# A transformer block in float32 parts: three quarters of a feed-forward product by seven products for eight

## The chip, the core and the metric

The kernel runs on one core of a Trainium2 chip. The metric is the time of one execution on the device in microseconds (us), the median of several runs.

## What is computed

Two layers of a hybrid block on 512 tokens of 1024 features, and after them two more mixers (a latent attention and a gated linear recurrence) that the change doesn't touch. A layer of the block, cut to what matters here:

```python
mixed = ga * (ya @ w_proj_att) + gb * (yb @ w_proj_mlstm)
x = x + mixed @ w_out
h2 = rms_norm(x, norm_mlp_w)
x = x + jnp.square(jax.nn.relu(h2 @ w_ff1)) @ w_ff2
```

Here ya is the output of a dilated attention and yb that of an mLSTM. w_ff1 is 1024 x 4096, w_ff2 is 4096 x 1024. The second feed-forward product, the last line's right one, is what the change rewrites.

## The kernel before, in words

All large products are made exact enough by parts. A float32 operand v becomes hi + lo, two float32r tiles: ScalarE copies v to hi, VectorE subtracts (`split`, lines 246 and 247). A product is then three matmuls, hi hi, hi lo and lo hi (`mm3`, lines 275 to 277). Each has 128 x 128 stationary elements and mostly 512 moving columns, and adds up in a bank of PSUM.

Weights come as units of 128 x 1024 float32, 512 KB, in the order in which they are used (`stream`, line 252). SP loads a unit into one of two tiles `raw` (line 259), and a split puts its parts into one of four tiles `spl`.

There are two shapes of product. A "tall" one keeps a weight unit still and moves the activations: 8 k x 3 = 24 matmuls give 128 features of all 512 tokens, in one bank A. A "wide" one keeps 128 tokens of an activation still and moves 512 columns of weights: `add_wide` (line 733) calls `halves` and `wide_acc`, and for each of two column halves and four token tiles 4 k x 3 = 12 matmuls fill a bank A, which VectorE adds into the residual x (line 737). There are two banks A; the attention uses three S, two T and one O besides.

The feed-forward stage of a layer runs over blocks b of 512 hidden features. For b below 8 there are four tall steps: one unit of w_ff1 each, relu on ScalarE (line 678), square on VectorE (line 679), and a split into `fs[b]`, a tile `big` of 16 KB a partition. After the first block each turn also does the wide product of block b - 1, 96 matmuls and four units of w_ff2. Between them stand uses of the modulation (lines 812 to 819): three VectorE sums over a unit of other weights that ScalarE's queue loads, 24 a layer.

The tiles `big` have five places. big0 to big2 lie in a pool that outlives the block and is opened on the left side of the on-chip memory; big3 and big4 lie in the pool `rest`, opened on the right side, so at its far end. fs uses the places 3, 4, 2 in turn; ya and yb lie in 3 and 4. The residual x, `raw`, `spl` and the constants are opened first, on the left.

Nobody writes the order of the work out by hand. The program lists it, and a planner lays each engine's queue down once, by the order of the program and its own estimate of what is ready and which places are free; on the chip each queue then runs in that order and waits on semaphores. Work without a place to wait for can so move far ahead: the modulation runs well before the feed-forward stage in which it is listed.

Of the kernel before, what the change touches and what calls it, by code (L numbers as in the profile page):

```python
# [24 lines left out]
# column groups of w_in  # L25
C_AQ, C_AK, C_AV, C_MQ, C_MK, C_MV, C_MO = (512 * i for i in range(7))
C_MI = 3584
C_GA, C_GB = 3592, 4616


# ------------------------------------------------------------------ host layout

def _tall(w, c0, n=128):
# [15 lines left out]
def pack_layer(a, l):  # L49
# [12 lines left out]
    for b in range(9):  # L62
        if b < 8:
            u += [_tall(f1, 512 * b + 128 * j) for j in range(4)]
        if b:
            for ch in range(2):
                u += [_wide(f2, 4 * (b - 1) + k, 512 * ch) for k in (0, 2)]
    return np.stack(u)

# [20 lines left out]
    # two heads' columns without position; four heads' that turn, first halves before second ones  # L90
# [36 lines left out]
def constants():  # L127
    i = np.arange(128)
    c = {"ident": np.eye(128, dtype=np.float32)}
    # multiplicity of a key at distance d in the three dilated patterns, as a logarithm  # L130
# [29 lines left out]
def layout(a):  # L160
    m = {}
    for l in range(2):
        m[f"wl{l}"] = pack_layer(a, l)
        m[f"cl{l}"] = pack_cols(a, l)
# [21 lines left out]
# ------------------------------------------------------------------ the program  # L186
# [5 lines left out]
class Prog:  # L192
    def __init__(self, tc, A, ctx):
        self.tc, self.nc, self.A, self.ctx = tc, tc.nc, A, ctx
        self.const = self.pool("const", 1)
        self.res = self.pool("res", 1)
        self.raw = self.pool("raw", 2)
# [15 lines left out]
    def rows(self, pool, ap, n, name, **kw):  # L213
        """A row of DRAM on every partition."""
# [4 lines left out]
    def psum(self, st, **banks):  # L219
        """Pools of PSUM: name -> (tiles, banks of a tile)."""  # L220
# [21 lines left out]
    # exact parts: x = hi + lo, each in float32r  # L242
# [47 lines left out]
def rms(P, dst, x, row, junk):  # L290
    """dst = x / rms(x) row"""
# [6 lines left out]
def act_of(tiles):  # L298
    """k -> (hi, lo) of a split, transposed activation kept four k to a tile."""
# [3 lines left out]
def trig_tables(P, ck):  # L303
    """sin and cos of the rope: token on partitions, [4 token tiles, 8 heads, 8 frequencies]."""
    nc = P.nc
    pos = P.load(ck, "pos", [128, 4], "pos", I32)
    inv = P.load(ck, "k_inv", [128, 8], "inv")
    posf = ck.tile([128, 4], F32, name="posf")
    nc.vector.tensor_copy(posf, pos)
    ang = ck.tile([128, 2, 4, 8], F32, name="ang")  # L310
# [6 lines left out]
    rn = ck.tile([128, 2, 4, 8], F32, name="rn")  # L317
# [14 lines left out]
def first_block(P, xs, pool):  # L332
# [1176 lines left out]
```

## Time and profile before

| what | us |
|---|---|
| median of 3 runs | 2382.06 |
| lowest, highest run | 2379.44, 2382.68 |
| span of the profiled execution, first to last instruction | 2376.0 |
| TensorE busy | 2336.0 |
| VectorE busy | 1438.8 |
| ScalarE busy | 961.2 |
| GpSimd busy | 48.5 |

The profile is of one execution; of its own time the span is what it records, and 6.1 us lie between that span and the median of the runs. Busy time counts an engine as busy from the start to the end of each instruction. Matmuls overlap, so their durations add up to more than they cost: the distance between two starts is the price of one. The feed-forward stages, from the first relu of line 678 to the last addition into x of line 737, are at about 440 to 792 us and 1217 to 1577 us.

### The profile page before, as it was taken

The page shows a single profiled execution, that of the slowest core. Times are in us where ns is not written, and L with a number is a line of the kernel's source. Part 1 is how long each engine was busy: PE and PEld are TensorE (multiplying, and loading weights), DVE is VectorE, ACT ScalarE, POOL GpSimd, SP SyncE. Part 2 cuts the span into 40 slices and gives each one's busy share as a digit, 9 for nine tenths or more (in the row PEclk, how much of TensorE's full clock was granted, in tenths as well). Part 3 has the DMA queues.
Part 4 walks back from the last instruction along what each step waited for, and adds up shares of the span by engine and source line. Part 5 has one row for each costly group of instructions (what it writes and reads, how often), then busy time and mean ns, then how long its engine had stood idle before and what let it go on. Part 6 is the DMA issues. An engine that isn't in the chain of part 4 may idle for free.

```text
span 2376.0 us, 30969 instructions
## 1 busy us (share of the span) xinstructions
PE 2336.0 (98%) x12280; PEld 1904.2 (80%) x12280; DVE 1438.8 (61%) x2534; ACT 961.2 (40%) x1809; POOL 48.5 (2%) x96
## 2 busy tenths in 40 slices
PE   8999999999999999999999999999999999999998
PEld 6777888888888777788888888789888888788886
DVE  4477795544444547779654444454477776647486
ACT  3356422422322226642342232333366783363332
POOL 0000000000000000000000000010000000000000
PEclk9999999999999999999999999999999999999999
DMA  4221463222323222146432222312110130121111
GB/s 152 80 82 48 166 215 124 92 94 89 106 89 99 83 80 72 54 152 215 136 106 98 89 98 98 97 39 89 45 28 19 24 88 22 59 88 36 48 51 71
DMA packets 61345, 209.24 MB, mean 88 GB/s; under 512 B 8576, under 2 KB 9872, under 8 KB 60944
## 3 DMA queue, kind: packets, MB, share of 16 engines
q1 hardware_dynamic: 54000, 179.99, 23.4%
q10 hardware_dynamic: 7200, 27.27, 3.5%
q8 instruction: 97, 1.59, 0.3%
q14 instruction: 48, 0.39, 0.1%
HBM read 201.99 MB, written 2.10 MB: 86 GB/s over the span
## 4 chain that ended last, share of the span: by engine, by line
PE 84%; DVE 8%; ACT 3%; DMA 2%; issue 2%; POOL 1%; SPq 0%; ACTq 0%; POOLq 0%; DVEq 0%
PE A L277 22%; PE A L276 22%; PE A L275 21%; PE O L1133 2%; PE T L1125 2%; DVE spl L247 2%; PE S L275 1%; PE O L512 1%; PE S L276 1%; PE S L277 1%; PE S L486 1%; DMA ada<-in_ada 1%; PE T L506 1%; DVE junk L817 1%; ACT spl L246 1%
## 5 line engine op out<-in xcount | busy, mean ns | idle before, releaser
L246 ACT ACTIVATE spl<-raw 128x1024 fp32r<-128x1024 f32 (+2 forms) x313 | 325.0, 1040 | 477.0 <-PE A L277 429.6
L275 PE MATMUL A<-big,spl 128*128 128x512 f32 (+1 forms) x1280 | 483.0, 377 | 1.9 <-DVE x L737 1.2
L277 PE MATMUL A<-big,spl 128*128 128x512 f32 (+1 forms) x1280 | 481.4, 376 | 0.2 <-DVE spl L247 0.2
L276 PE MATMUL A<-big,spl 128*128 128x512 f32 (+1 forms) x1280 | 480.8, 376 | 0.0
L247 DVE TENSOR_TENSOR spl<-raw,spl 128x1024 fp32r<-128x1024 f32 (+2 forms) x313 | 375.8, 1204 | 163.1 <-ACT spl L246 161.7
L276 PE MATMUL A<-spl,big 128*128 128x512 f32 (+2 forms) x992 | 384.7, 389 | 1.1 <-DVE spl L247 1.0
L275 PE MATMUL A<-spl,big 128*128 128x512 f32 (+2 forms) x992 | 383.6, 388 | 1.6 <-ACT big L246 0.8
L277 PE MATMUL A<-spl,big 128*128 128x512 f32 (+2 forms) x992 | 381.8, 385 | 0.2 <-DVE ms L284 0.2
L277 PEld LDWEIGHTS A<-big,spl 128*128 128x128 f32 x1280 | 241.1, 188 | 45.9 <-issue 2.6
L275 PEld LDWEIGHTS A<-big,spl 128*128 128x128 f32 x1280 | 241.2, 188 | 45.1 <-DVE x L737 1.6
L276 PEld LDWEIGHTS A<-big,spl 128*128 128x128 f32 x1280 | 241.2, 188 | 43.3 <-issue 1.4
L275 PEld LDWEIGHTS A<-spl,big 128*128 128x128 f32 x992 | 186.3, 188 | 44.2 <-ACT big L246 2.8
L276 PEld LDWEIGHTS A<-spl,big 128*128 128x128 f32 x992 | 186.7, 188 | 40.3 <-DVE spl L247 3.0
L277 PEld LDWEIGHTS A<-spl,big 128*128 128x128 f32 x992 | 186.6, 188 | 39.2 <-issue 1.5
L737 DVE SCALAR_TENSOR_TENSOR x<-A,x 128x512 f32<-128x512 f32 x160 | 110.0, 688 | 121.7 <-PE A L277 119.9
L679 DVE TENSOR_TENSOR r<-r 128x512 f32<-128x512 f32 (+1 forms) x72 | 45.5, 633 | 170.9 <-ACT r L678 170.9
L678 ACT ACTIVATE r<-A 128x512 f32<-128x512 f32 (+1 forms) x72 | 39.7, 551 | 219.8 <-PE A L277 219.6
L1100 DVE TENSOR_REDUCE mx<-S 128x1 f32<-128x768 f32 (+1 forms) x80 | 71.8, 900 | 26.7 <-PE S L277 25.8
L1126 ACT ACTIVATE pt<-T 128x512 f32<-128x512 f32 (+1 forms) x144 | 66.5, 501 | 32.2 <-PE T L1125 31.1
L286 POOL TENSOR_TENSOR rstd<-ms,mhalf 128x1 f32<-128x1 f32 (+2 forms) x68 | 42.4, 623 | 1765.1 <-DVE ms L284 1720.8
L1105 ACT ACTIVATE p<-S,mx 128x768 f32<-128x768 f32 (+1 forms) x96 | 72.6, 760 | 13.8 <-DVE mx L1100 12.9
L817 DVE SCALAR_TENSOR_TENSOR junk<-ada,cond 128x512 f32<-128x512 f32 x96 | 65.7, 687 | 6.1 <-DMA ada<-in_ada 4.9
(413 smaller groups left out, 3438.8 us busy)
## 6 DMA issues: line engine op xcount, KB each, us to landing
raw<-in_wl SPq DMA_DIRECT2D x244, 512.0 KB, 3.2
ada<-in_ada ACTq DMA_DIRECT2D x48, 512.0 KB, 3.8
raw<-in_gla SPq DMA_DIRECT2D x33, 512.0 KB, 3.2
raw<-in_mla SPq DMA_DIRECT2D x20, 512.0 KB, 3.3
raw<-in_mla SPq DMA_DIRECT2D x8, 384.0 KB, 2.9
qT<-rot SPq DMA_DIRECT2D x32, 96.0 KB, 2.8
x<-in_x SPq DMA_DIRECT2D x4, 512.0 KB, 10.2
big<-in_wl SPq DMA_DIRECT2D x4, 512.0 KB, 9.3
```

What stands on the lines that cost most here:

```text
L246: nc.scalar.activation(hi, src, AF.Copy)
L247: nc.vector.tensor_tensor(lo, src, f32(hi), op=OP.subtract)
L275: mm(ps, lh, rh, start=start, stop=False)
L276: mm(ps, lh, rl, start=False, stop=False)
L277: mm(ps, ll, rh, start=False, stop=stop)
L737: P.nc.vector.scalar_tensor_tensor(xv, ps, scale, xv, op0=OP.mult, op1=OP.add)
L817: nc.vector.scalar_tensor_tensor(junk, w[:, o], 0.5, self.cond[:, 0, o], op0=OP.mult, op1=OP.mult, accum_out=self.acc[:, g, j:j + 1])
L1100: nc.vector.tensor_reduce(mx[:, 0:two], pss[:, 0:two * m].rearrange("p (t n) -> p t n", t=two), AX.X, OP.max, negate=True)
L1105: nc.scalar.activation(p[:, t * m:(t + 1) * m], pss[:, t * m:(t + 1) * m], AF.Exp, bias=mx[:, t:t + 1], accum_out=sl[:, t:t + 1])
L1125: nc.tensor.transpose(pst[:, k:k + 128], p[:, o + k:o + k + 128], P.ident)
L1126: nc.scalar.activation(pt[:, o:o + w], pst[:, 0:w], AF.Copy)
L1133: nc.tensor.matmul(weigh.o[64 * i:64 * i + 64, (t0 + t) * 128:(t0 + t + 1) * 128], V[4 * c + k][:, h * 64:(h + 1) * 64], pts[i][:, t * m + ...
```

## The change

In the first 3072 of the 4096 hidden features, six of the eight blocks, two blocks and all 512 tokens make a chunk. A chunk is a product of a 2 x 2 matrix of activation quarters (256 tokens by 512 features: a11, a12, a21, a22) with a 2 x 2 matrix of weight quarters (512 by 512, 1 MB: b11 and so on). The new class `Seven` computes it by seven products of sums of quarters. The activation sums are VectorE's (`total`). The weight sums are made where the quarter lies, by DMAs that GpSimd issues and that add to what is there (`accum_op`), four a chunk. The sums of products that are shared are kept in the banks S and O: X and Y are two banks each, products are added to what they hold, and VectorE adds each state of a bank to its place in x with a sign. SP loads four quarters a chunk into four places, in turn.

The activations stay as float32 when the features are made (relu and square both on ScalarE); a product splits the sum that it takes (`part`), and its two weight units, as it needs them. Feature steps and products alternate: a tall step, then one of the seven products of the chunk before. The last two blocks stay as wide products, with four activation parts. Each tall step of the first three of a group of four also lists one use of the modulation.

The pools move: x and `raw` go to the right side, the pool `rest` with big3 and big4 to the left, closed before the feed-forward stage, where `parts`, `quarter` and `hidden` take its place. The buffer for GpSimd's DMA descriptors is set to 1024 bytes a partition.

```diff
@@ pack_layer, pack_quarters
-    for b in range(9):
-        if b < 8:
-            u += [_tall(f1, 512 * b + 128 * j) for j in range(4)]
-        if b:
-            for ch in range(2):
-                u += [_wide(f2, 4 * (b - 1) + k, 512 * ch) for k in (0, 2)]
+    u += [_tall(f1, 128 * j) for j in range(32)]
+    for b in (6, 7):
+        for ch in range(2):
+            u += [_wide(f2, 4 * b + k, 512 * ch) for k in (0, 2)]
     return np.stack(u)
+def pack_quarters(a, l):
+    w = a["w_ff2"][l][0:3072].reshape(3, 2, 4, 128, 2, 512).transpose(0, 1, 4, 3, 2, 5)
+    return np.stack([w[:, i, j] for i, j in QUARTERS], axis=1).reshape(12, 128, 2048)
...
@@ Prog
-        self.res = self.pool("res", 1)
-        self.raw = self.pool("raw", 2)
+        self.res = self.pool("res", 1, side="right")
+        self.raw = self.pool("raw", 2, side="right")
...
@@ mm3
-    def mm3(self, ps, lh, ll, rh, rl, start, stop):
+    def mm3(self, ps, lh, ll, rh, rl, start, stop, **more):
         mm = self.nc.tensor.matmul
-        mm(ps, lh, rh, start=start, stop=False)
-        mm(ps, lh, rl, start=False, stop=False)
-        mm(ps, ll, rh, start=False, stop=stop)
-    # ---- residual stream -> normalised, transposed, split
+        mm(ps, lh, rh, start=start, stop=False, **more)
+        mm(ps, lh, rl, start=False, stop=False, **more)
+        mm(ps, ll, rh, start=False, stop=stop, **more)
...
@@ act_of, cut
+def cut(a):
+    return lambda t, k: tuple(v[:, t * 128:(t + 1) * 128] for v in a(k))
...
@@ first_block, pools
-    rest = P.pool("big", 1, st, side="right")
-    def big(i, dtype=F32R):
-        """Five places, three of them in the pool that outlives this block."""
-        return (pool if i < 3 else rest).tile([128, 2, 4, 512], dtype, name="big", tag=f"big{i}")
-    vp = P.pool("vp", 1, st)
-    tmp = P.pool("tmp", 2, st)
-    one = P.pool("one", 1, st)
-    pp = P.pool("pp", 3, st)
-    ck = P.pool("ck1", 1, st)
+    ck = P.pool("ck1", 1, st, side="right")
+    vp = P.pool("vp", 1, st, side="right")
     for l in range(2):
+        mixing = ExitStack()
+        rest = P.pool("big", 1, mixing)
+        tmp, one, pp = (P.pool(n, k, mixing) for n, k in (("tmp", 2), ("one", 1), ("pp", 3)))
+        def big(i, dtype=F32R):
+            return (pool if i < 3 else rest).tile([128, 2, 4, 512], dtype, name="big", tag=f"big{i}")
...
@@ first_block, feed-forward
+        mixing.close()
+        mod.start(l, vp)
         act2 = act_of(norm.dst)
-        mod.start(l, vp)
-        fs = {}
-        for b in range(9):
-            if b < 8:
-                fs[b] = big((3, 4, 2)[b % 3])
-                ws = [W() for _ in range(4)] if b == 0 else None
-                for n0, n1 in ((0, 256), (256, 512)) if b == 0 else ((0, 512),):
+        after = ExitStack()
+        parts = P.pool("parts", 3, after)
+        quarter, hid = P.pool("quarter", 1, after), P.pool("hidden", 1, after)
+        tmp, one = (P.pool(n, k, after) for n, k in (("tmp2", 3), ("one2", 1)))
+        seven = Seven(P, xs, A[f"wq{l}"], parts, quarter, tmp)
+        def features(c):
+            f = fs[c] = big(2, F32) if c % 2 == 0 else hid.tile([128, 2, 4, 512], F32, name="hidden")
+            for i in range(2):
+                ws = [W() for _ in range(4)] if c + i == 0 else None
+                for n0, n1 in ((0, 256), (256, 512)) if c + i == 0 else ((0, 512),):
                     for j in range(4):
                         ps = P.bankA()
                         tall(ps, ws[j] if ws else W(), act2, range(8), n0, n1)
-                        r = tmp.tile([128, 512], F32, name="r", tag="yf")[:, n0:n1]
+                        r = f[:, i, j, n0:n1]
                         nc.scalar.activation(r, ps[:, n0:n1], AF.Relu)
-                        nc.vector.tensor_tensor(r, r, r, op=OP.mult)
-                        P.split(fs[b][:, 0, j, n0:n1], fs[b][:, 1, j, n0:n1], r)
-            for g in range(24 * b // 9, 24 * (b + 1) // 9):
-                mod.use(l, g, tmp, "u")
-            done = None
-            if b == 7 and l == 1:
-                # what the mixer after this block takes of ctx
+                        nc.scalar.activation(r, r, AF.Square)
+                        yield
+        fs, chunks = {}, iter(range(24))
+        for c in range(4):
+            more = seven.chunk(c - 1, fs[c - 1]) if c else iter(())
+            for i, _ in enumerate(features(c)):
+                if i % 4 < 3:
+                    for g in itertools.islice(chunks, 1):
+                        mod.use(l, g, vp, "junk")
+                next(more, None)
+            for _ in more:
+                pass
+        for g in chunks:
+            mod.use(l, g, vp, "junk")
+        last = [[seven.part(seven.of(fs[3], i, j), *((quarter, "quarter1") if i + j == 2 else ())) for i in range(2)]
+                for j in range(2)]
+        done = None
+        for j in range(2):
...
-            if b == 8:
+            if j == 1:
...
-            if b:
-                add_wide(P, W, act_of([fs.pop(b - 1)]), xs, 1.0, done)
+            add_wide(P, W, lambda t, k: seven.cut(last[j][t // 2], t % 2, k), xs, 1.0, done)
+        after.close()
...
@@ wide_acc, Seven
-def wide_acc(P, ps, us, a, t, nk):
+def wide_acc(P, ps, us, still, t, nk):
     for k in range(nk):
-        hi, lo = a(k)
         u = us[k // 2].rearrange("p s (k n) -> p s k n", k=2)
-        P.mm3(ps, hi[:, t * 128:(t + 1) * 128], lo[:, t * 128:(t + 1) * 128],
-              u[:, 0, k % 2], u[:, 1, k % 2], k == 0, k == nk - 1)
+        P.mm3(ps, *still(t, k), u[:, 0, k % 2], u[:, 1, k % 2], k == 0, k == nk - 1)
+class Seven:
+    def __init__(self, P, xs, units, parts, quarter, tmp):
+        self.P, self.xs, self.units, self.parts, self.quarter, self.tmp = P, xs, units, parts, quarter, tmp
+        self.n = 0
+        self.X, self.Y = [P.bankS(), P.bankS()], [P.bankS(), P.bankO()]
+    @staticmethod
+    def of(f, i, j):
+        return f[:, j, :, 256 * i:256 * i + 256]
+    def part(self, src, pool=None, tag="part"):
+        u = (pool or self.parts).tile([128, 2, 4, 256], F32R, name="part", tag=tag)
+        self.P.split(u[:, 0], u[:, 1], src)
+        return u
+    @staticmethod
+    def cut(u, t, k):
+        return u[:, 0, k, t * 128:(t + 1) * 128], u[:, 1, k, t * 128:(t + 1) * 128]
+    def product(self, ps, a, b, start, to):
+        P, nc = self.P, self.P.nc
+        u, ws = self.part(a), []
+        for i in range(2):
+            w = P.spl.tile([128, 2, 1024], F32R, name="spl")
+            P.split(w[:, 0], w[:, 1], b[:, i * 1024:(i + 1) * 1024])
+            ws.append(w.rearrange("p s (k n) -> p s k n", k=2))
+        for t in range(2):
+            for k in range(4):
+                w = ws[k // 2]
+                P.mm3(ps[t], *self.cut(u, t, k), w[:, 0, k % 2], w[:, 1, k % 2], start and k == 0, k == 3, skip_group_check=not start)
+            r, c, sign = to
+            x = self.xs[2 * r + t][:, 512 * c:512 * c + 512]
+            nc.vector.scalar_tensor_tensor(x, ps[t], sign, x, op0=OP.mult, op1=OP.add)
+    def place(self):
+        self.n += 1
+        return f"quarter{self.n % 4}"
+    def chunk(self, c, f):
+        nc = self.P.nc
+        units = [self.units[4 * c + i] for i in range(4)]
+        q = {}
+        for i in (0, 2, 1, 3):
+            q[i] = self.quarter.tile([128, 2048], F32, name="quarter", tag=self.place())
+            nc.sync.dma_start(q[i], units[i])
+        self.n += 1
+        b11, b12, b22, b21 = (q[i] for i in range(4))
+        a11, a12, a21, a22 = (self.of(f, i, j) for i in range(2) for j in range(2))
+        def add(b, i):
+            nc.gpsimd.dma_start(b, units[i], accum_op=OP.add)
+        def total(x, y, op):
+            v = self.tmp.tile([128, 4, 256], F32, name="total", tag="qm")
+            nc.vector.tensor_tensor(v, x, y, op=op)
+            return v
+        self.product(self.X, a11, b11, True, (0, 0, 1.0))
+        yield
+        add(b11, 1)
+        d = total(a21, a22, OP.subtract)
+        self.product(self.Y, d, b11, True, (1, 1, 1.0))
+        yield
+        add(b11, 2)
+        s = total(d, a11, OP.subtract)
+        self.product(self.X, s, b11, False, (0, 1, -1.0))
+        yield
+        s = total(a12, s, OP.add)
+        self.product(self.Y, s, b22, False, (0, 1, 1.0))
+        yield
+        add(b12, 2)
+        self.product(self.X, total(a11, a21, OP.subtract), b12, False, (1, 1, -1.0))
+        yield
+        add(b11, 3)
+        self.product(self.Y, a12, b21, True, (0, 0, 1.0))
+        yield
+        self.product(self.X, a22, b11, False, (1, 0, 1.0))
...
@@ kernel
-    nc = bacc.Bacc("TRN2", target_bir_lowering=False, num_devices=1)
+    nc = bacc.Bacc("TRN2", target_bir_lowering=False, num_devices=1, dynamic_dma_scratch_size=1024)
```

Elsewhere the diff only takes comments out, passes `still(t, k)` where `a(k)` was cut, and moves small tiles (the trigonometry's) to another pool.

## Rows read from the trace of the kernel before

**Rows 1.** The page: busy time by engine, and the granted clock in 40 slices.

```profile
PE 2336.0 (98%) x12280; PEld 1904.2 (80%) x12280; DVE 1438.8 (61%) x2534; ACT 961.2 (40%) x1809; POOL 48.5 (2%) x96
...
PEclk9999999999999999999999999999999999999999
```

**Rows 2.** Windows: from:to us, length, busy us of each engine (count), clock, DMA share, GB/s.

```profile
280.00:320.00 40.00, 40.00 (x176) 32.61 (x174) 38.24 (x77) 11.58 (x14) 0.00 (x0) 1.00 0.69 222
480.00:520.00 40.00, 40.00 (x176) 32.53 (x175) 17.53 (x21) 10.45 (x13) 0.00 (x0) 1.00 0.31 103
560.00:600.00 40.00, 40.00 (x178) 33.11 (x177) 19.20 (x24) 11.43 (x15) 0.00 (x0) 1.00 0.28 93
```

**Rows 3.** Groups by line, 440 to 790 us: engine, operation, count | busy, mean ns | idle, releaser.

```profile
L275 PE MATMUL A<-spl,big 128*128 128x512 f32 x255 | 100.2, 393 | 0.0
...
L247 DVE TENSOR_TENSOR spl<-raw,spl 128x1024 fp32r<-128x1024 f32 x62 | 75.8, 1223 | 35.0 <-ACT spl L246 35.0
L246 ACT ACTIVATE spl<-raw 128x1024 fp32r<-128x1024 f32 x62 | 65.5, 1057 | 118.4 <-PE A L277 118.3
...
L737 DVE SCALAR_TENSOR_TENSOR x<-A,x 128x512 f32<-128x512 f32 x63 | 43.4, 688 | 58.7 <-PE A L277 57.9
```

**Rows 4.** Who waited for whom, 440 to 790 us: total us, times, longest.

```profile
POOL rstd L286 <- DVE ms L284: 350.9, 3, 339.9
ACT spl L246 <- PE A L277: 118.3, 27, 8.8
ACT r L678 <- PE A L277: 110.0, 34, 4.4
```

**Rows 5.** Timeline of TensorE, activations in big3: start us, us, operation.

```profile
482.63 0.39 PE L275 MATMUL A<-spl,big 128*128 128x512 f32 x1
...
485.43 0.39 PE L275 MATMUL A<-spl,big 128*128 128x512 f32 x1
```

**Rows 6.** Timeline of TensorE, activations in big2.

```profile
569.63 0.39 PE L275 MATMUL A<-spl,big 128*128 128x512 f32 x1
...
572.35 0.39 PE L275 MATMUL A<-spl,big 128*128 128x512 f32 x1
```

**Rows 7.** Timeline of TensorE, projection with the moving operand in big3 or big4.

```profile
402.86 0.40 PE L275 MATMUL A<-big,spl 128*128 128x512 f32 x1
...
405.66 0.40 PE L275 MATMUL A<-big,spl 128*128 128x512 f32 x1
```

**Rows 8.** Timeline of ScalarE, last feature step and a wide product.

```profile
569.89 0.60 ACT L678 ACTIVATE r<-A 128x512 f32<-128x512 f32 x1 [3.38 <-PE A L277]
570.38 1.05 ACT L246 ACTIVATE spl<-raw 128x1024 fp32r<-128x1024 f32 x1
571.33 0.62 ACT L246 ACTIVATE big<-r 128x512 fp32r<-128x512 f32 x1
579.35 1.06 ACT L246 ACTIVATE spl<-raw 128x1024 fp32r<-128x1024 f32 x1 [7.39 <-PE A L277]
580.71 1.06 ACT L246 ACTIVATE spl<-raw 128x1024 fp32r<-128x1024 f32 x1 [0.30 <-PE A L277]
```

**Rows 9.** The modulation's instructions by their lines: duration ns, first and last start.

```profile
L817 DVE SCALAR_TENSOR_TENSOR junk<-ada,cond x48: 677/687/695, 268.6 to 369.5; 128x512 f32<-128x512 f32 x48
L817 DVE DVE_READ_ACCUMULATOR junk<-ada,cond x48: 78/82/86, 269.2 to 370.1; 128x1 f32 x48
```

**Rows 10.** The modulation's third sum, group by line, whole span.

```profile
L819 DVE SCALAR_TENSOR_TENSOR ada<-ada,cond 128x1024 f32<-128x1024 f32 x48 | 58.6, 1221 | 1.0
```

**Rows 11.** DMA issues: tile, queue, count, KB each, median us from issue to landing.

```profile
raw<-in_wl SPq DMA_DIRECT2D x244, 512.0 KB, 3.2
ada<-in_ada ACTq DMA_DIRECT2D x48, 512.0 KB, 3.8
...
x<-in_x SPq DMA_DIRECT2D x4, 512.0 KB, 10.2
```

More of the change, by code (lines that the diff above doesn't have):

```diff
@@ L28 @@
 C_GA, C_GB = 3592, 4616
+QUARTERS = ((0, 0), (0, 1), (1, 1), (1, 0))
 def _tall(w, c0, n=128):
@@ L163, in layout @@
         m[f"wl{l}"] = pack_layer(a, l)
+        m[f"wq{l}"] = pack_quarters(a, l)
         m[f"cl{l}"] = pack_cols(a, l)
@@ L300, in act_of, with trig_tables @@
     return lambda k: (tiles[k // 4][:, 0, k % 4], tiles[k // 4][:, 1, k % 4])
-def trig_tables(P, ck):
+def cut(a):
+    return lambda t, k: tuple(v[:, t * 128:(t + 1) * 128] for v in a(k))
+def trig_tables(P, ck, one):
     nc = P.nc
-    pos = P.load(ck, "pos", [128, 4], "pos", I32)
-    inv = P.load(ck, "k_inv", [128, 8], "inv")
-    posf = ck.tile([128, 4], F32, name="posf")
+    pos = P.load(one, "pos", [128, 4], "pos", I32)
+    inv = P.load(one, "k_inv", [128, 8], "inv")
+    posf = one.tile([128, 4], F32, name="posf")
     nc.vector.tensor_copy(posf, pos)
-    ang = ck.tile([128, 2, 4, 8], F32, name="ang")
+    ang = one.tile([128, 2, 4, 8], F32, name="ang")
     nc.vector.tensor_tensor(ang[:, 0], posf[:, :, None].to_broadcast([128, 4, 8]),
@@ L316, in trig_tables @@
     p3 = 2.0 * math.pi - p1 - p2
-    rn = ck.tile([128, 2, 4, 8], F32, name="rn")
+    rn = one.tile([128, 2, 4, 8], F32, name="rn")
     magic = 12582912.0
@@ L374, in first_block @@
         act = act_of(norm.dst)
+        still = cut(act)
         cl = P.load(tmp, f"cl{l}", [128, 73], "cl")
@@ L388, in wide_z @@
                 ps = P.bankA()
-                wide_acc(P, ps, us, act, t, 8)
+                wide_acc(P, ps, us, still, t, 8)
                 evac(t, ps, b)
@@ L405, in first_block @@
             if l == 0 and i == 0:
-                sin_b, cos_b = trig_tables(P, ck)
+                sin_b, cos_b = trig_tables(P, ck, one)
             if i < 2:
@@ L662, in first_block @@
                 norm = Norm(P, xs, A["norm_mlp_w"][l], one, tmp, big)
-            add_wide(P, W, act_of([mx_T]), xs, 0.5, norm if kh else None)
+            add_wide(P, W, cut(act_of([mx_T])), xs, 0.5, norm if kh else None)
+        mixing.close()
+        mod.start(l, vp)
         act2 = act_of(norm.dst)
-        mod.start(l, vp)
-        fs = {}
-        for b in range(9):
-            if b < 8:
-                fs[b] = big((3, 4, 2)[b % 3])
-                ws = [W() for _ in range(4)] if b == 0 else None
-                for n0, n1 in ((0, 256), (256, 512)) if b == 0 else ((0, 512),):
+        after = ExitStack()
[8 more added lines that the diff above has]
+                for n0, n1 in ((0, 256), (256, 512)) if c + i == 0 else ((0, 512),):
                     for j in range(4):
@@ L676, in first_block @@
                         tall(ps, ws[j] if ws else W(), act2, range(8), n0, n1)
-                        r = tmp.tile([128, 512], F32, name="r", tag="yf")[:, n0:n1]
+                        r = f[:, i, j, n0:n1]
                         nc.scalar.activation(r, ps[:, n0:n1], AF.Relu)
-                        nc.vector.tensor_tensor(r, r, r, op=OP.mult)
-                        P.split(fs[b][:, 0, j, n0:n1], fs[b][:, 1, j, n0:n1], r)
-            for g in range(24 * b // 9, 24 * (b + 1) // 9):
-                mod.use(l, g, tmp, "u")
-            done = None
-            if b == 7 and l == 1:
+                        nc.scalar.activation(r, r, AF.Square)
[16 more added lines that the diff above has]
+        for j in range(2):
+            if j == 0 and l == 1:
                 H = Tokens(*(big(i) for i in (2, 0, 1)))
@@ L773, in both @@
                 yield
-def wide_acc(P, ps, us, a, t, nk):
+def wide_acc(P, ps, us, still, t, nk):
     for k in range(nk):
-        hi, lo = a(k)
         u = us[k // 2].rearrange("p s (k n) -> p s k n", k=2)
-        P.mm3(ps, hi[:, t * 128:(t + 1) * 128], lo[:, t * 128:(t + 1) * 128],
-              u[:, 0, k % 2], u[:, 1, k % 2], k == 0, k == nk - 1)
+        P.mm3(ps, *still(t, k), u[:, 0, k % 2], u[:, 1, k % 2], k == 0, k == nk - 1)
[67 more added lines that the diff above has]
+        self.product(self.X, a22, b11, False, (1, 0, 1.0))
+        yield
@@ L1180, in finish @@
         for kh in range(2):
-            halves(P, W, lambda k: (hi[4 * kh + k], lo[4 * kh + k]), TILES, evac,
+            halves(P, W, cut(lambda k: (hi[4 * kh + k], lo[4 * kh + k])), TILES, evac,
                    (lambda t: done(t, place(t))) if kh else None)
@@ L1454, in output @@
         yield
-        a, us = act_of([oT]), {}
+        a, us = cut(act_of([oT])), {}
         order = [(ch, t) for ch in range(2) for t in range(4)]
```

## The prediction

> **What bounds the kernel now.** I began with the page's table of engines and its slices: TensorE is busy 98% of the span, VectorE 61%, ScalarE 40%, and the granted clock is 9 tenths or more in every slice [rows 1], so nothing can be won from the clock. Busy time says little about price here, since a matmul is shown with 0.39 us and the next one starts after 0.23. So I went on to the stretch that is changed, the feed-forward stage of layer 0, from about 440 to 790 us. Its windows show TensorE busy for all 40.00 of 40 us, VectorE for 17.5 to 19.2, ScalarE for 10.5 to 11.4, the DMA engines at a share of 0.28 to 0.31 [rows 2]. The groups of that stretch name no releaser in front of the matmuls, and both helpers wait for TensorE: ScalarE's splits 118.3 us, its relu 110.0 [rows 3, 4]. A stage with one engine that never stops and the others half idle is bounded by the count of matmuls times the distance of their starts. That distance I read from the timeline. In the second product it is (485.43 - 482.63) / 12 = 0.2333 us where the stationary tile is big3 or big4, and (572.35 - 569.63) / 12 = 0.2267 us where it is big2 [rows 5, 6]. big3 and big4 are the tiles of the pool `rest`, opened on the right; big2 lies in the pool on the left.
>
> **Part 1: fewer matmuls.** The second product is 8 blocks x 8 banks x 12 matmuls = 768 a layer, 1536 in all. The change makes 6 of the 8 blocks into 3 chunks; a chunk has 7 products of 2 token tiles x 4 k x 3 = 24 matmuls, 168 for 192. Removed are 24 x 3 x 2 = 144. At 0.2267 us: 144 x 0.2267 = **32.6 us**.
>
> **Part 2: where the operands lie.** Of a layer's 8 blocks, b = 0, 1, 3, 4, 6, 7 use big3 or big4: 6 x 96 x 2 = 1152 matmuls at the slow distance. The change puts x, raw, ck1 and vp on the right and `rest` on the left; by the tile sizes in the code it then ends near 116 KB, and the new `parts` pool stands in the same place. I take all at big2's distance: 1152 x (0.2333 - 0.2267) = **7.7 us**. The projections of ya and yb, which are big3 and big4, move in the other operand and show the same (405.66 - 402.86) / 12 = 0.2333 [rows 7]: 2 x 8 x 2 x 12 = 384 of these, **2.6 us**. Bounds: nothing, if the distance follows something else than the place; 10.3 for both. I take 10.3, since two kinds of operand in the same pool show the same distance.
>
> **Part 3: what the other engines get.** Per chunk, TensorE runs 8 feature steps and 7 products of 24 x 0.2267 = 5.44 us each: 81.6 us. VectorE gets 8 + 14 halves of weight splits and 7 of activation parts, 29 x 1.22, four sums of the same 128x1024 shape, 4 x 1.22, and 14 additions into x, 14 x 0.69 [rows 3]: 35.4 + 4.9 + 9.7 = 50 us. The square leaves it for ScalarE, where it takes the place of the small split, 0.62 beside a relu of 0.60 [rows 8]. ScalarE: 29 x 1.06 + 8 x (0.60 + 0.62) = 40.5 us. Both stay well under 81.6, so these cost nothing as long as TensorE hides them. The modulation, 24 uses of 2 x 0.69 + 2 x 0.08 + 1.22 = 2.8 us, ran at 268.6 to 369.5 us, before this stage [rows 9, 10]; should it fall in here, 6 uses a chunk make VectorE 67 us, still under. The weights: 8 MB plainly and 4 MB by the accumulating loads in 81.6 us is 154 GB/s; the stretch with the modulation's loads moved 222 at a share of 0.69 [rows 2]. The banks S and O that X and Y take stand idle in this stage. The last two blocks are split as 4 parts of 1024 (4 x 1.06 us on ScalarE) instead of 8 of 512; the first two parts need features that are done four steps earlier, and the other two have the 96 matmuls of j = 0 as cover, 21.8 us: nothing.
>
> **Part 4: the new wait.** This is the only term that the trace can't give. The quarter b11 is loaded, split for product 1, then added to by a DMA that GpSimd issues, split for product 2, added to again, and split for product 3. Each addition must wait for both engines' reads, and the next split for its landing. Cover is found from the order of the splits: a unit's split starts as TensorE leaves a spl place (in the wide product at 579.35 and 580.71 us, each released by a matmul) [rows 4, 8], and there are 4 places; a product takes 2, a feature step 1. Let time 0 be the end of the previous product 7. Then F8 and F1 run to 10.9, P1 to 16.3, F2 to 21.8, P2 to 27.2, F3 to 32.6, where P3 starts. P1's second unit gets its place at 0 and is split by 2.4 (1.06 + 1.22 and the gap). Let L be the time from there to the landing. P2's second unit gets the place that P1's first unit leaves after 18 of its 24 matmuls, at 15.0, so P2's splits end at 17.4, or at 2.4 + L + 3.4 if that is later. P3's first unit must have landed at 32.6 - 2.3 = 30.3. There is no stall up to L = 12.2; above that TensorE waits 2L - 24.5 us in each of 6 chunks. Meanwhile ScalarE's next split stands at the head of its queue; behind it wait the relu that frees bank A and F3's split, and for those TensorE. GpSimd has nothing else queued in this stage but its rstd at the end [rows 4]. SP's four loads a chunk wait for a place of a quarter and hold up the raw units behind them, whose landing of 3.2 us lies inside a step of 5.44: nothing.
>
> For L the nearest rows are plain loads of 512 KB: 3.2 us for a raw unit, 3.8 for the modulation's, 10.2 at worst, for x at the start, among others [rows 11]. An addition moves 1 MB: 6.4 us by twice the raw unit; 12.8 if what it adds to has to be read as well; 20.4 by x's landing. The stalls are 0, 6 x 1.1 = 6.6, and 6 x 16.3 = 98 us. I take the middle of the first two as the price, **3.3 us**, because the DMA share here is nearer the raw unit's surroundings than x's. A gain is excluded, for nothing waited here before.
>
> By the Trainium skill (DMA: Bandwidth & Descriptors, Anatomy of one DMA) a GpSimd-issued DMA lasts about 2.0 us plus bytes / 436 GB/s, and (Collectives: The Full Stack, The bandwidth ceiling) an addition in flight reads two sources on the same ring, which halves its rate; an estimate from both pages is 2.0 + 2 x 2.4 = 6.8 us, and by that the stall would be zero and the sum 3.3 us lower. No row of this trace has such a DMA.
>
> **Sum.** 32.6 + 10.3 - 3.3 = 39.6 us less. Against the profiled execution that is a span of 2376.0 - 39.6 = 2336.4. The median of the runs, 2382.06, lies 6.1 above that span; what lies around it is left as it is: 2382.1 - 39.6 = **2342.5 us**.
>
> **Rivals.**
> (a) *The place of the tiles does nothing.* Against it stand two operand kinds with one distance; for it, that no row shows an address. Then all 144 are saved at their old mix, 108 x 0.2333 + 36 x 0.2267 = 33.4, less 3.3: 2352.0.
> (b) *The additions come late but not ruinously*, L of 13 to 15.5: 1.5 to 6.5 us a chunk, 9 to 39 us, which leaves 2348 to 2378. For it: the chain of two landings sits in two steps of 10.9 us each, and the DMA queues are fuller than before. Against: 12.2 is nearly four times the raw unit's landing.
> (c) *Slower*: the same chain, with a landing like x's at the start. It decides from 2L - 24.5 = 42.9 / 6, so L = 15.8; at 20.4 the stalls take 98 us: 2382.1 - 42.9 + 98 = 2437. For it: such a DMA is not in the trace, and its two landings follow each other with nothing to overlap them. Against: 222 GB/s were moved in the modulation's stretch at 3.8 us a landing.
> (d) *Nothing in sum*, with the same stalls eating just the gain: 2377 to 2387.
>
> **Chances.** Forecast 0.56 (2334 to 2348), (a) 0.08, (b) 0.15, (d) 0.06, (c) 0.15. A measurement of this kernel can tell 0.2%, 4.8 us, from no change. Forecast, (a) and (b) are faster: 0.79; (d) is the same: 0.06; slower 0.15. The range goes from 2333 (all of 42.9, and 6 us for runs that lie lower and operands of the later stages that move left too) up to 2374, which takes in (a) and most of (b); (d), (c) and the rest of (b) lie outside.
>
> **What would show it.** Feature steps and products that follow each other by 5.44 us, and a distance of 0.2267 in all matmuls of the two layers' second product; 144 matmuls fewer; no idle time on TensorE in front of product 2 or 3 of a chunk. Wrong would be: ScalarE's split or VectorE's waiting for the landing of a quarter by more than TensorE's lead; windows of 40 us in this stage in which TensorE isn't busy for all 40; a distance of 0.2333 on the `parts` tiles; VectorE above 90% in the stage.

## The result and the profile after

The changed kernel takes **2336.76 us** (median of 4 runs, 2336.23 to 2337.96) against 2382.37 of the kernel before (4 runs, 2379.44 to 2382.89): a ratio of 0.9815, interval 0.9802 to 0.9828, 45.6 us less. 2342.5 were forecast, in a range of 2333 to 2374.

The page of the kernel after, busy time by engine and granted clock, answers to [rows 1]. Its DMA issues (tile, queue, count, KB each, median us from issue to landing) answer to [rows 11]; the second `quarter` row is the accumulating DMA, which the kernel before did not have:

```profile
PE 2294.2 (98%) x12136; PEld 1877.7 (80%) x12136; DVE 1467.6 (63%) x2488; ACT 1047.2 (45%) x1895; POOL 69.5 (3%) x120
...
PEclk9999999999999999999999999999999999999999
...
raw<-in_wl SPq DMA_DIRECT2D x196, 512.0 KB, 3.5
ada<-in_ada ACTq DMA_DIRECT2D x48, 512.0 KB, 4.2
quarter<-in_wq SPq DMA_DIRECT2D x24, 1024.0 KB, 6.3
quarter<-in_wq POOLq DMA_DIRECT2D x24, 1024.0 KB, 8.8
```

TensorE has 12280 - 12136 = 144 matmuls fewer, and is busy for the same 98%. Next the windows that answer to [rows 2]: VectorE and ScalarE have taken the splits of parts and quarters, the DMA share has doubled, and TensorE still works 40.00 of 40 us in the two windows of the feed-forward stage.

```profile
280.00:320.00 40.00, 39.26 (x175) 32.17 (x173) 38.18 (x77) 12.28 (x15) 0.00 (x0) 1.00 0.69 220
480.00:520.00 40.00, 40.00 (x179) 33.10 (x178) 25.62 (x25) 20.88 (x25) 1.77 (x2) 1.00 0.61 152
560.00:600.00 40.00, 40.00 (x178) 33.11 (x177) 25.61 (x25) 19.48 (x23) 2.37 (x3) 1.00 0.61 145
```

The timeline of TensorE at the first chunk of layer 0 and, in its first two rows, at a projection of ya or yb. It answers to [rows 5 to 7]:

```profile
402.17 0.39 PE L281 MATMUL A<-big,spl 128*128 128x512 f32 x1
...
404.89 0.39 PE L281 MATMUL A<-big,spl 128*128 128x512 f32 x1
...
485.77 0.39 PE L281 MATMUL S<-spl,part 128*128 128x512 f32 x1
...
496.65 0.39 PE L281 MATMUL S<-spl,part 128*128 128x512 f32 x1
...
499.37 0.39 PE L281 MATMUL O<-spl,part 128*128 128x512 f32 x1
...
502.09 0.39 PE L281 MATMUL A<-big,spl 128*128 128x512 f32 x1
...
507.53 0.39 PE L281 MATMUL S<-spl,part 128*128 128x512 f32 x1
```

Products 1, 2 and 3 start at 485.77, 496.65 and 507.53; between 2 and 3 a feature step starts at 502.09. Each is 5.44 us, without a gap. Twelve matmuls on the `part` tiles take 499.37 - 496.65 = 2.72 us, 0.2267 each, and so do twelve with ya or yb, (404.89 - 402.17) / 12, where the kernel before had 0.2333.

By stages (from the first relu of a layer to its last addition into x) the profiled execution is 20.2 and 20.3 us shorter in the two feed-forward stages, 0.8 and 0.9 in what stands ahead of each (the projections of ya and yb among it), and 1.6 longer behind the second: 40.7 us, 2376.0 to 2335.3.

The new wait is in the timelines of ScalarE and of VectorE, for the same chunk:

```profile
490.05 1.07 ACT L252 ACTIVATE spl<-quarter 128x1024 fp32r<-128x1024 f32 x1 [1.28 <-PE S L283]
...
503.11 2.01 ACT L252 ACTIVATE spl<-quarter 128x1024 fp32r<-128x1024 f32 x2 [5.00 <-DMA quarter<-in_wq]
```

```profile
492.52 1.21 DVE L253 TENSOR_TENSOR spl<-quarter,spl 128x1024 fp32r<-128x1024 f32 x1
...
504.20 2.36 DVE L253 TENSOR_TENSOR spl<-quarter,spl 128x1024 fp32r<-128x1024 f32 x2 [3.95 <-ACT spl L252]
```

Then GpSimd's, at the addition between products 2 and 3:

```profile
494.03 0.87 POOL L874 DMA_DIRECT2D quarter<-in_wq  x1 [14.95 <-DVE spl L253]
```

VectorE ends product 2's splits at 492.52 + 1.21 = 493.73, GpSimd issues the addition at 494.03, and it lands at 503.1. ScalarE's split stood 5.00 us at the head of its queue for it; VectorE is done with both units at 506.6, and product 3 starts at 507.53 on time. The waits between 440 and 760 us, which answer to [rows 4] (total us, times, longest), show how seldom that is, three times:

```profile
ACT hidden L697 <- PE A L283: 43.6, 13, 4.4
...
ACT spl L252 <- DMA quarter<-in_wq: 16.2, 3, 6.1
```

No row of that view has TensorE waiting.

### The profile page after: what moved, and what is told of

It is laid out like the page before. It is cut to its first block, busy times and chain, and to the rows that moved or that the text cites. A ratio compares the mean times of both kernels' runs of the same rounds, so it can differ in the third digit from the quotient of the medians.

```text
span 2335.3 us, 30710 instructions
## 1 busy us (share of the span) xinstructions
PE 2294.2 (98%) x12136; PEld 1877.7 (80%) x12136; DVE 1467.6 (63%) x2488; ACT 1047.2 (45%) x1895; POOL 69.5 (3%) x120
## 4 chain that ended last, share of the span: by engine, by line
PE 83%; DVE 8%; ACT 3%; DMA 2%; issue 2%; POOL 1%; SPq 0%; ACTq 0%; POOLq 0%; DVEq 0%
PE A L283 18%; PE A L282 18%; PE A L281 18%; PE S L281 4%; PE S L282 4%; PE S L283 4%; PE O L1252 2%; PE T L1244 2%; DVE spl L253 2%; PE O L523 1%; DMA ada<-in_ada 1%; PE S L497 1%; DVE junk L936 1%; PE T L517 1%; ACT spl L252 1%
## 5 line engine op out<-in xcount | busy, mean ns | idle before, releaser
L253 DVE TENSOR_TENSOR spl<-raw,spl 128x1024 fp32r<-128x1024 f32 (+2 forms) x265 | 317.3, 1200 | 183.1 <-ACT spl L252 181.4
L252 ACT ACTIVATE spl<-raw 128x1024 fp32r<-128x1024 f32 (+2 forms) x265 | 274.2, 1037 | 299.3 <-PE A L283 198.4
L253 DVE TENSOR_TENSOR spl<-quarter,spl 128x1024 fp32r<-128x1024 f32 x84 | 102.2, 1223 | 143.5 <-ACT spl L252 143.5
L281 PE MATMUL A<-spl,big 128*128 128x512 f32 (+2 forms) x480 | 182.0, 383 | 3.8 <-DVE tg L669 2.1
L282 PE MATMUL A<-spl,big 128*128 128x512 f32 (+2 forms) x480 | 182.1, 380 | 0.9 <-DVE spl L253 0.8
L283 PE MATMUL A<-spl,big 128*128 128x512 f32 (+2 forms) x480 | 181.3, 379 | 0.2 <-DVE ms L290 0.2
L252 ACT ACTIVATE spl<-quarter 128x1024 fp32r<-128x1024 f32 x84 | 88.2, 1057 | 97.4 <-PE S L283 40.9
L281 PEld LDWEIGHTS A<-spl,big 128*128 128x128 f32 x480 | 90.1, 189 | 23.1 <-ACT big L252 3.0
L282 PEld LDWEIGHTS A<-spl,big 128*128 128x128 f32 x480 | 90.6, 189 | 18.7 <-DVE spl L253 2.7
L283 PEld LDWEIGHTS A<-spl,big 128*128 128x128 f32 x480 | 90.5, 189 | 16.9 <-issue 1.3
L281 PE MATMUL S<-spl,part 128*128 128x512 f32 x264 | 102.7, 389 | 0.0
L282 PE MATMUL S<-spl,part 128*128 128x512 f32 x264 | 102.7, 389 | 0.0
L283 PE MATMUL S<-spl,part 128*128 128x512 f32 x264 | 102.7, 389 | 0.0
```

What stands on the lines that cost most here:

```text
L252: nc.scalar.activation(hi, src, AF.Copy)
L253: nc.vector.tensor_tensor(lo, src, f32(hi), op=OP.subtract)
L281: mm(ps, lh, rh, start=start, stop=False, **more)
L282: mm(ps, lh, rl, start=False, stop=False, **more)
L283: mm(ps, ll, rh, start=False, stop=stop, **more)
```

## The experiments

Times are medians; "after again" below is 2338.1. The kernel before ran beside each of these kernels, at 2379.5 to 2381.5.

**Both kernels again.** No edit.

> The kernel before once more, unchanged, to see how its span and its time lie to each other. The profile of before has a span of 2376.0 us, the median of its runs is 2382.4, 6.4 above; in the four runs of the changed kernel the time lies 1.8 above the span. Theory 1: the profiled execution of before was a fast one of its kind, and its span is usually near 2380.5 (time less 1.8). Theory 2: something around the span costs the kernel before 4.6 us more than the changed one, and its span is again 2376.

> The changed kernel once more, unchanged, beside the others of this call: 2336.8 us within 2, span 1.8 below the time. It is what the next two are compared with.

Measured: before 2380.13 (2377.61 to 2382.78, 10 runs), ratio 1.0 (0.9991 to 1.0009), profiled span 2378.5; after 2338.1 (2336.58 to 2338.93), ratio 0.9821 (0.9808 to 0.9834). In every run of these experiments the time lies 1.7 to 1.9 us above the span. So the profiled execution of the kernel before, 2376.0 + 1.8, was a quick one of a kernel that scatters over 5 us; 6.1 us around a span do not exist.

**The places alone, in the kernel before.** The right side for x, `raw`, vp and ck1, the left for `rest` (and the 1024 bytes for GpSimd's descriptors, as in the change):

```diff
-        self.res = self.pool("res", 1)
-        self.raw = self.pool("raw", 2)
+        self.res = self.pool("res", 1, side="right")
+        self.raw = self.pool("raw", 2, side="right")
...
-    rest = P.pool("big", 1, st, side="right")
+    rest = P.pool("big", 1, st)
```

> The kernel before with only the pools moved (x, raw, ck1 and vp to the right, rest to the left, the descriptor buffer at 1024 bytes), all products as before. Theory: the place of an operand sets the distance of matmuls; all 1152 + 384 matmuls on big3 and big4 go from 0.2333 to 0.2267 us, 10.3 us less than before, about 2372. Rival: the place does nothing, and the whole gain of the change is in the seven products: within 1 us of before, distances of 0.2333 on the tiles of rest as before.

Measured: 2372.11 (2370.27 to 2377.21), ratio 0.9966 (0.9954 to 0.9977): 7 to 8 us, with all matmuls on big3 and big4 at a median of 227 ns. That is most of the 10.3 that Part 2 had for the move; why not all is not shown. Whether the side did it was the next run.

**The far side, in the kernel after.**

```diff
-        rest = P.pool("big", 1, mixing)
+        rest = P.pool("big", 1, mixing, side="right")
...
-        parts = P.pool("parts", 3, after)
+        parts = P.pool("parts", 3, after, side="right")
```

> The changed kernel with the pools rest and parts opened on the right side. Theory of place: 1296 matmuls on parts and 384 on ya and yb go from 0.2267 to 0.2333 us, 8.6 + 2.6 = 11.2 us more than the changed kernel, about 2348. Rival, that the place does nothing: 2336.8 within 1 us.

Measured: 2336.5 (2335.44 to 2338.71), ratio 0.9817 (0.9804 to 0.9831). The three places of `parts` now start at 158528 to 174912 bytes of a partition of the on-chip memory, and 12 matmuls on them still take 498.63 - 495.91 = 2.72 us, 0.2267 each:

```profile
495.91 0.39 PE L281 MATMUL S<-spl,part 128*128 128x512 f32 x1
...
498.63 0.39 PE L281 MATMUL O<-spl,part 128*128 128x512 f32 x1
```

**Neither the side nor how far up the tiles lie is the cause.** The place matters (the run before this one), but not as near or far.

**No additions, and every addition twice.** Of `add`, the DMA left out, or

```diff
-            nc.gpsimd.dma_start(b, units[i], accum_op=OP.add)
+            for _ in range(2):
+                nc.gpsimd.dma_start(b, units[i], accum_op=OP.add)
```

> The changed kernel without the accumulating loads: the products take the plain quarters, so three quarters of the second feed-forward product come out as another sum; everything else is as in the changed kernel. Theory: in the changed kernel's trace the split for product 2 stands ready 9 us ahead of TensorE and that for product 3 some 2 us, so the loads are wholly hidden and leaving them out gains nothing: 2337 within 2 us. Rival: they cost by their traffic (25 MB more, raw units landing in 3.5 for 3.2 us) or by waits elsewhere: at least 3 us faster.

> The changed kernel with every accumulating load made twice in a row, the second waiting for the first, so the weight sums hold a quarter twice and the product is another sum; the rest is the same. In the changed kernel 10.6 us pass from the end of product 2's splits to the landing (492.5 to 503.1 us); twice makes L about 20. Theory of the prediction: TensorE waits 2L - 24.5 = 16 us in each of 6 chunks, 96 us more, about 2433, in front of products 2 and 3. Rival 1: the planner sees the longer chain and puts feature steps in front, so that less than half of that is lost. Rival 2: there is more cover than the prediction counted, and the time stays within 5 us of 2337.

Measured without: 2338.24 (2336.36 to 2338.66), ratio 0.9821 (0.9807 to 0.9834), as after again: the additions are wholly hidden. Measured twice: 2427.47 (2424.59 to 2428.4), ratio 1.0195 (1.0181 to 1.0209): 89.4 us more than after again, on the mean 14.9 in each of the 6 chunks. First the timeline of TensorE with double additions, at product 3 of the first chunk; then that of ScalarE; then the window behind the stall:

```profile
508.78 0.39 PE L283 MATMUL A<-big,spl 128*128 128x512 f32 x1
518.26 0.80 PE L281 MATMUL S<-spl,part 128*128 128x512 f32 x1 [9.10 <-ACT spl L252]
519.52 0.80 PE L282 MATMUL S<-spl,part 128*128 128x512 f32 x1 [0.46 <-DVE spl L253]
```

```profile
517.15 2.00 ACT L252 ACTIVATE spl<-quarter 128x1024 fp32r<-128x1024 f32 x2 [12.33 <-DMA quarter<-in_wq]
519.06 1.04 ACT L252 ACTIVATE spl<-raw 128x1024 fp32r<-128x1024 f32 x1
520.01 0.58 ACT L697 ACTIVATE hidden<-A 128x512 f32<-128x512 f32 x1
```

```profile
518.00:526.00 8.00, 7.28 (x19) 5.49 (x20) 5.32 (x5) 4.05 (x6) 0.87 (x1) 0.58 0.46 77
```

This is rival (c) brought about: the split at the head of ScalarE's queue, behind it the raw split and the relu, and TensorE idle for 9.10 us. The gaps in TensorE's timeline behind its first instruction add up to 92.9 us against 22.7 in the kernel after: 70 of the 89 us, 11.7 a chunk. The other 19, 3.2 a chunk, come behind the stalls: the matmul after one is shown with 0.80 us for 0.39, and the window behind this one shows a granted clock of 0.58, so for most of it the lower of the two levels, 1.2 for 2.4 GHz, and holds 19 matmuls in 8 us, where 8 / 0.2267 = 35 fit. What the engine did before is the idle stretch above.

**All four quarters of the second product by seven products.** The last chunk has no feature steps left beside it, so its products follow each other in another order (1, 6, 2, 4, 3, 5, 7):

```diff
-    w = a["w_ff2"][l][0:3072].reshape(3, 2, 4, 128, 2, 512).transpose(0, 1, 4, 3, 2, 5)
+    w = a["w_ff2"][l].reshape(4, 2, 4, 128, 2, 512).transpose(0, 1, 4, 3, 2, 5)
...
+        more = seven.chunk(3, fs[3], last=True)
...
+        for _ in range(4):
+            next(more)
```

> The changed kernel with all four quarters of the second feed-forward product by seven products; the last chunk has no feature steps between its products, and runs them in the order 1, 6, 2, 4, 3, 5, 7, so that 6 and 4 cover the two landings and the first 256 tokens are done two products early. 48 matmuls fewer: 48 x 0.2267 = 10.9 us. Theory: two products of 5.44 us cover 10.6 us of landing but for the split, so at most 2 us a layer is lost, and the norm of the first tokens runs beside products 5 and 7: 2326 to 2330. Rival: without feature steps the last chunk waits for its landings and its splits, 5 us or more a layer, and nothing is won: 2335 or more.

Measured: 2349.46 (2348.86 to 2350.96), ratio 0.9869 (0.9855 to 0.9882): 48 matmuls fewer than after, and 11.4 us slower. 48 x 0.2267 = 10.9 should have gone, so 22 were lost. The gaps in TensorE's timeline are 40.8 us for 22.7, and most of the 18 more lie in front of one product in each layer, 5.58 and 9.39 us; the clock goes down behind them, as with the double additions, to a mean of 0.80 over the 8 us from 763 and from 1531. Timeline of TensorE in the last chunk of layer 1, then that of ScalarE:

```profile
1521.04 0.39 PE L280 MATMUL S<-spl,part 128*128 128x512 f32 x1
1530.82 0.79 PE L278 MATMUL S<-spl,part 128*128 128x512 f32 x1 [9.39 <-ACT part L249]
```

```profile
1525.32 2.00 ACT L249 ACTIVATE spl<-quarter 128x1024 fp32r<-128x1024 f32 x2 [3.46 <-DMA quarter<-in_wq]
1527.23 1.04 ACT L296 ACTIVATE xn<-x 128x1024 f32<-128x1024 f32 x1
...
1529.71 1.06 ACT L249 ACTIVATE part<-total 128x1024 fp32r<-128x1024 f32 x1 [0.31 <-DVE total L881]
```

With no feature steps between the products the addition lands too late; ScalarE waits for it, and behind it stand the norm of the next stage and the parts of the product that TensorE needs. The wait for the landing itself is 3.46 of the 9.39 us; the splits of that quarter, two steps of the norm and the parts behind them take the rest. So feature steps are cover that the fourth quarter lacks, but the edit also changes the order of the products and puts the norm among them, and how the loss divides between these was not tested.

**What is it in the place?** A tile starts at some byte of each partition; the build of the program sets it, and no profile shows it. The starts of the tiles that were fast had one thing in common. In the kernel after `big2` starts at 69696 and `rest` at 86080, in the far one `rest` at 150336: all 64 bytes past a multiple of 256. The slow `rest` of the kernel before started at 196576, 224 past one. Four runs shift tiles by small pads, each a tile that nothing else uses. In the kernel before, 32 and then 160 bytes, first on the right side:

```diff
+        self.pad = self.pool("pad", 1, side="right").tile([128, 8], F32, name="pad")
...
```

(`[128, 40]` in the second.) In the kernel after, 32 bytes ahead of `rest` and of `parts`, and then 64 and 128:

```diff
+        off = P.pool("off", 1, mixing).tile([128, 8], F32, name="off")
...
         rest = P.pool("big", 1, mixing)
...
+        off = P.pool("off2", 1, after).tile([128, 8], F32, name="off2")
...
         parts = P.pool("parts", 3, after)
```

> The kernel before with one tile of 32 bytes opened first on the right, so that rest and the later right-hand pools start 32 bytes lower and at a multiple of 64 bytes (196544 for 196576), still at the far end. With rest and parts on the right in the changed kernel, at 150336 and 158528, multiples of 64, the distance was 0.2267 us, so it isn't the side. Theory of alignment: the 1536 matmuls on big3 and big4 go to 0.2267 us, 10.3 us less, and some of the 600 slow ones on the right-hand tiles of the latent attention gain 0.0067 us each too, up to 4 us: 2366 to 2370. Rival, that the far end of the memory is slow (above 192 KB): no change, 2379.5 within 1.5 us.

> The changed kernel with 32 bytes in front of rest and of parts, on the left, so that these start 32 bytes after a multiple of 64 (86112 for 86080). Theory of alignment: 1392 matmuls on parts and 384 on ya and yb go from 0.2267 to 0.2333 us, 11.8 us more: about 2349. Rival, that a place at the near end is fast whatever its last bits: 2337 within 1.5 us.

> The kernel before with a tile of 160 bytes opened first on the right: rest starts at 196416. So far fast tiles (0.2267 us) started at 36928, 53312, 69696, 86080, 102464, 150336, 158528 and so on, all 64 more than a multiple of 256; slow ones (0.2333) at 196576 and 212960 (224 more), 86112 (96 more), and after the shift by 32 at 196544 and 212928 (192 more). 196416 is 64 more than a multiple of 256, like the fast ones. Theory of residue (where a start lies modulo 128 or 256 decides): 10.3 us less than before, about 2369. Theory of two conditions (a multiple of 64, and not the far end above some 183 KB): no change, 2380 within 2 us.

> The changed kernel with 64 bytes in front of rest (86144, 128 more than a multiple of 256) and 128 in front of parts (86208, 192 more). Theory of residue modulo 256: the 1392 matmuls on parts become slow as those at 196544 were, 9.3 us more, about 2346 to 2349. Theory of two conditions: both are multiples of 64 at the near end, so all stays at 0.2267 us, 2337 within 2 us.

Measured, with the start of each operand's tile modulo 256 and the median distance to the next start, from all matmuls of the kind in each trace (1152 with `rest` or 1392 on `part` tiles, 384 with ya or yb; `spl`, the split weights, starts 64 past):

| kernel | other operand starts past 256 | distance ns: products, ya and yb | us | ratio |
|---|---|---|---|---|
| before + 32 | 192 | 232, 234 | 2378.56 | 0.9991 (0.9982 to 1.0) |
| before + 160 | 64 | 227, 227 | 2370.0 | 0.9953 (0.9941 to 0.9966) |
| after + 32 | 96 | 232, 234 | 2348.97 | 0.9868 (0.9853 to 0.9883) |
| after + 64, 128 | parts 192, ya and yb 128 | 232, 229 | 2346.1 | 0.9852 (0.9837 to 0.9867) |

A start at a multiple of 64 bytes is not enough: in the first row it is one, and the matmuls stay slow. And a shift of 160 bytes in the kernel before gives 11 us with nothing else changed. Here are 12 matmuls in each timeline: of the kernel before with 32 bytes, then with 160, then of the kernel after with 32:

```profile
483.11 0.39 PE L277 MATMUL A<-spl,big 128*128 128x512 f32 x1
...
485.90 0.40 PE L277 MATMUL A<-spl,big 128*128 128x512 f32 x1
```

```profile
480.88 0.39 PE L277 MATMUL A<-spl,big 128*128 128x512 f32 x1
...
483.60 0.39 PE L277 MATMUL A<-spl,big 128*128 128x512 f32 x1
```

```profile
500.68 0.40 PE L281 MATMUL S<-spl,part 128*128 128x512 f32 x1
...
503.48 0.40 PE L281 MATMUL O<-spl,part 128*128 128x512 f32 x1
```

They take 2.79, 2.72 and 2.80 us: 0.2325, 0.2267 and 0.2333 each. But in all these `spl` starts 64 past 256 as well. It could be that 64 is the good place, or that both operands have to start alike.

**Both operands moved together.** In the kernel after, 128 bytes ahead of everything on the left, 32 on the right:

```diff
+        self.off = self.pool("off", 1).tile([128, 32], F32, name="off")
+        self.pad = self.pool("pad", 1, side="right").tile([128, 8], F32, name="pad")
         self.const = self.pool("const", 1)
...
```

> The kernel after, with every tile of the left side moved up by 128 bytes (a small tile in a pool opened first) and the right side moved down by 32: the split weights, the activations and the parts, which all started 64 bytes past a multiple of 256, now all start 192 past one, and so do the right-hand tiles of the latent attention, which started 224 past one. Nothing else changes. Theory A (an operand must start 64 past a multiple of 256): both operands of nearly all wide matmuls are now in the slow place, some 2,000 to 9,000 of them lose 5 to 7 ns each: 2350 to 2400 us, and distances of 0.232 to 0.235 in the feature steps, products and projections. Theory B (the two operands must start alike modulo 256, wherever that is): distances stay at 0.2267 in the products, and the right-hand tiles of the latent attention, some 300 to 600 wide matmuls, go from 0.232 to 0.238 down to 0.227: 2334 to 2337 us, against 2338.1 of the kernel after.

Measured: **2334.16** (2333.17 to 2335.11), ratio 0.9803 (0.979 to 0.9817), where theory A had 2350 at least. Theory B holds: `spl`, the activations, the parts and the right-hand tiles start 192 past 256, and all wide matmuls of products and projections stay at 227 ns. The latent attention, whose tiles `hi` and `lo` lie on the right, gains. There the timeline of TensorE of the kernel after has

```profile
1950.35 0.40 PE L281 MATMUL A<-spl,hi 128*128 128x512 f32 x1
...
1953.15 0.40 PE L281 MATMUL A<-spl,hi 128*128 128x512 f32 x1
```

and that of this kernel

```profile
1950.38 0.39 PE L285 MATMUL A<-spl,hi 128*128 128x512 f32 x1
...
1953.10 0.39 PE L285 MATMUL A<-spl,hi 128*128 128x512 f32 x1
```

2.80 and 2.72 us for 12: 0.2333 and 0.2267. From the first matmul on `hi` to the last the profiled execution takes 1.7 us less than that of the kernel after, and behind it 1.4 less. This is the fastest of the kernels run; its lead over after is 2.6 to 3.9 us, but the two did not run side by side, and the intervals of their ratios overlap.

## Why the prediction was right, and where it was not

**What bounds the kernel: right.** TensorE does not stop in the feed-forward stages, and count times distance is their time. VectorE at 25.6 and ScalarE at 20.9 of 40 us stay below.

**Part 1: right.** 144 matmuls fewer. Parts 1 and 2 together forecast (32.6 + 7.7) / 2 = 20.2 us for a feed-forward stage; 20.2 and 20.3 were measured between the profiled executions.

**Part 2: the amount about right, the reason wrong.** Forecast were 10.3 us for tiles that leave the right side. All of them came to 0.2267; the move alone gave 7 to 8 us and the pad of 160 bytes, which brings the right-hand tiles of the latent attention along, 11. But the step "big3 and big4 are the tiles of the pool `rest`, opened on the right" took the side for the cause. With `rest` and `parts` on the right the distance stayed at 0.2267, and 32 bytes on the left brought 0.2333 back. What the runs show in its place: the two operands' tiles have to start alike modulo 256 bytes. The change made them so by the sizes of its pools, and that is luck: with 32 bytes more in front of them 11 us of the gain were gone. Rival (a) was the right kind of doubt, "no row shows an address", with the wrong outcome here. What stands ahead of the feed-forward stages became 0.8 and 0.9 shorter for the 1.3 forecast in each layer, but this says little: when the kernel before ran again, its first relu came 1.9 us later. Rival (a)'s 108 and 36 are the mix of all eight blocks; in the six that the change takes it is 96 and 48, which moves its 33.4 us by 0.1.

**Part 3: right.** The modulation again ran before the stage (its window from 280 us stands above, like that of [rows 2]), and VectorE's 25.6 and ScalarE's 20.9 of 40 us are near the 24.5 and 19.9 that 50 and 40.5 of 81.6 come to.

**Part 4: the formula right, its price not needed.** L, as defined there, runs from the end of a product's splits to the landing: 493.73 to 503.1 for product 2 of the first chunk, 9.4 us, and 8.3 to 10.5 in all chunks, for product 1 and product 2. That is under the threshold of 12.2, so the stall is zero and the 3.3 us were too much; without additions the time is the same. Double additions put the formula to the test above the threshold. There the landings came on the mean 16.9 us (product 1) and 18.4 us (product 2) after the end of the splits, for which it gives 16.9 + 18.4 - 24.5 = 10.8 us a chunk; TensorE's gaps are 11.7 a chunk. The 3.2 us of low clock behind them are not in the formula. That 14.9 in all came near the 16 expected of that run is luck: its L of 10.6 was read from the start of the last split, not from its end. An addition of 1 MB takes 8.8 us from issue to landing. By the Trainium skill (DMA: Bandwidth & Descriptors, Anatomy of one DMA; Collectives: The Full Stack, The bandwidth ceiling, which is about the additions of collectives) the prediction's estimate was 6.8; the trace is 2.0 longer, in a stage in which a plain load of as much takes 6.3, but the outcome that was worked out from it, no stall, is what came.

**The sum.** 39.6 us were forecast. The spans of the profiled executions differ by 40.7, but that of the kernel before was a quick one; the medians differ by 45.6, and by 42.0 when both kernels ran again (2380.13 to 2338.1). Without the 3.3 us for a stall the sum is 42.9, which lies among these. So the stall is the term of the sum that was mis-sized, 3.3 for nothing. Of the 5.7 us by which the median came out lower than forecast, the other 2.4 are within what the median of the kernel before differs by from one set of runs to the next, 2379.5 to 2382.4.

**The rivals.** (b), (c) and (d) needed a landing over 12.2 us. (c) is no phantom: it came with twice the additions, and the variant without feature steps beside the last chunk fell in part to the same wait.

## What to carry to other kernels

Where matmuls of one shape have two distances, look at the addresses of both operands before you look at their pools: a pad of some bytes that makes both tiles start alike modulo 256 took 11 us off the kernel before, and nothing in the code shows it. A saving in matmuls that needs operands made by a chain of DMAs is worth its count only with other matmuls as cover: find the landing that the cover stands for, as 12.2 us here. Above it expect to lose the excess of each landing in the chain, and a low clock on top: here 10.8 us by that formula, 11.7 of gaps and 3.2 at the lower clock.

## What the runs showed of the hardware that was not expected

A matmul of 128x128 by 128x512 starts 227 ns after the one before it when its two operands' tiles start alike modulo 256 bytes (64 and 64, or 192 and 192), and 229 to 234 ns on the median when they differ by 32, 64, 128 or 160 (64 was tried on the moving operand alone). It is so whether the stationary or the moving operand is the one that was moved, and whether the tiles lie near each other or far apart. What in the memory or in TensorE's reads does it is not shown. The Trainium skill (TensorE: Matmul & The Clock Gate, Part 2: What happens when you issue a matmul) says that TensorE has two independent read ports and that loading the next weights takes nothing from the running matmul. The runs here speak for a small cost of the one to the other, up to 7 ns in 227, that depends on both addresses; that it lies in the ports is only argued.
